# Rows of 256 columns without a gap, and operand tiles at whole 64 bytes, in a one-core encoder block

## The chip, the core and the metric

One core of a Trainium2 chip runs the program. The metric is the device time of one execution in microseconds. Three executions of the kernel before took 1994.06, 1997.44 and 2000.67; the median is 1997.44.

## What is computed

One layer over 256 tokens of width 2048, in float32: two gated feed-forward blocks (FFN) around a token mixer with a convolution group and a gated DeltaNet group. Norms and modulation stand ahead of each.

```python
h = modulate(rmsnorm(x, ffn1_norm[l]), mods[:, 0], mods[:, 1])
x = x + 0.5 * mods[:, 2][:, None, :] * swiglu(h, ffn1_wg[l], ffn1_wu[l], ffn1_wd[l])
h = modulate(rmsnorm(x, mix_norm[l]), mods[:, 3], mods[:, 4])
p = h @ w_in[l]
...
y = jnp.concatenate([y_conv, y_dn], axis=-1) @ w_out[l]
x = x + mods[:, 5][:, None, :] * y
h = modulate(rmsnorm(x, ffn2_norm[l]), mods[:, 6], mods[:, 7])
x = x + 0.5 * mods[:, 8][:, None, :] * swiglu(h, ffn2_wg[l], ffn2_wu[l], ffn2_wd[l])
return rmsnorm(x, final_norm)
```

## The kernel before

All arrays stand transposed: 128 features on the partitions, the 256 tokens along the free axis. A float32 product is made of three float32r matmuls: weights and activations are each split into a leading part (hi) and the rest (lo), and `mm3` (L139) adds hi by hi, hi by lo and lo by hi in PSUM. An activation tile therefore has two rows in a partition, the hi part and the lo part. In `act` tiles (`ffn_evac`, L287) they are two rows of 256 columns, 2048 bytes. In `h` tiles (`h_make` L232, `h_pre` L244, and the mixer's outputs at L568 and L824) they are two rows of 258 columns, 2064 bytes, of which mostly 256 are used; `h_pre` fills the two more with the shift, so that the matmuls of `group` (L260) yield a bias beside the product.

Weights arrive by DMA in `raw` tiles of 1 MB on the queue of SyncE (`load`, L118). `split` (L110) makes of each half a `hi` tile on ScalarE (L113) and a `lo` tile on VectorE (L115); there are four raw, three hi and three lo buffers. One pair of hi and lo carries 24 matmuls.

The stages in order: `first` (L388), the front part of FFN 1, in which the modulation weights still arrive (`ada`, L205) and h is made (L142 to L144, moving operand h); the rest of FFN 1's gate and up products in `col_pair` (L345, matmuls at L354, moving operand h) and its down products (L142 to L144, moving operand act), each in two halves, up to about 790 us; the mixer with `col_tile` (L338, L142 to L144, moving operand h) up to about 1240 us, with small plain float32 matmuls for the DeltaNet (L594 to L818) and seven plain float32 output products (L894); then FFN 2 like FFN 1. Both `group` stages stand at the head of the mixer and of FFN 2, with 258 columns.

The pools stand one behind the other in SBUF: pers, rawp, hip, lop, hp, tmp, small, and behind these the pools of a stage (act tiles, the mixer's tiles). Each tile is rounded up to 32 bytes. What stands in pers is made in `start` (L357), among it `prm` (L368, 593 floats) and the columns `col` and `col2` (L379, L381).

Of the kernel before, what the change touches and what calls it, by code (L numbers as in the profile page):

```python
# [8 lines left out]
F32 = mybir.dt.float32  # L9
F32R = mybir.dt.float32r  # L10
# [5 lines left out]
P = 128  # L16
T = 256
# [23 lines left out]
def spans(items):  # L41
    at, out = 0, {}
    for name, n in items:
        out[name] = slice(at, at + n)
        at += n
    return out, at


PSPAN, NPRM = spans(PARAMS)


class Body:
# [86 lines left out]
    def mm3(self, out, whi, wlo, rhs, start, stop):  # L139
        nc = self.nc  # L140
        rhi, rlo = rhs
        nc.tensor.matmul(out, lhsT=whi, rhs=rhi, start=start, stop=False)  # L142
        nc.tensor.matmul(out, lhsT=whi, rhs=rlo, start=False, stop=False)  # L143
        nc.tensor.matmul(out, lhsT=wlo, rhs=rhi, start=False, stop=stop)  # L144
# [87 lines left out]
    def h_make(self, k, rb, scale, shift, spare=None):  # L232
        nc = self.nc
        sh = self.mods[:, shift * 16 + k:shift * 16 + k + 1]
        h = self.tile(self.hp, [P, 2, T + 2], "h", F32R)
        t = spare() if spare else self.tile(self.tmp, [P, T], "ht")
        nc.vector.scalar_tensor_tensor(out=t, in0=self.x[:, k, :], scalar=self.mods[:, scale * 16 + k:scale * 16 + k + 1],  # L237
                                       in1=rb, op0=ALU.mult, op1=ALU.mult)
        nc.scalar.activation(out=h[:, 0, 0:T], in_=t, func=AF.Identity, bias=sh)
        nc.vector.scalar_tensor_tensor(out=h[:, 1, 0:T], in0=t, scalar=sh, in1=h[:, 0, 0:T].bitcast(F32),  # L240
                                       op0=ALU.add, op1=ALU.subtract)
        self.h[k] = h

    def h_pre(self, k, scale, shift):  # L244

        nc = self.nc
        sc = self.mods[:, scale * 16 + k:scale * 16 + k + 1]
        sh = self.mods[:, shift * 16 + k:shift * 16 + k + 1]
        h = self.tile(self.hp, [P, 2, T + 2], "h", F32R)
        nc.scalar.activation(out=h[:, 0, 0:T], in_=self.x[:, k, :], func=AF.Copy, scale=sc)  # L250
        nc.scalar.activation(out=h[:, 0, T:T + 2], in_=sh.broadcast_to([P, 2]), func=AF.Copy)
        nc.vector.scalar_tensor_tensor(out=h[:, 1, 0:T], in0=self.x[:, k, :], scalar=sc, in1=h[:, 0, 0:T].bitcast(F32),
                                       op0=ALU.mult, op1=ALU.subtract)
        nc.vector.tensor_tensor(out=h[:, 1, T:T + 2], in0=sh.broadcast_to([P, 2]), in1=h[:, 0, T:T + 2].bitcast(F32), op=ALU.subtract)
        self.h[k] = h
# [89 lines left out]
    def col_pair(self, ps, src):  # L345

        nc, kk = self.nc, 0
        for half in range(2):
            for hi, lo in self.weights(src[half]):
                for k in range(4):  # L350
                    rhi, rlo = self.rhs(self.h[kk])
                    for w, r, start, stop in ((hi, rhi, kk == 0, False), (hi, rlo, False, False), (lo, rhi, False, kk == 15)):
                        for g in range(2):
                            nc.tensor.matmul(ps[g], lhsT=w[:, 2 * k + g, :], rhs=r, start=start, stop=stop)  # L354
                    kk += 1

    def start(self):  # L357
        nc, pers = self.nc, self.pers
        self.ones = pers.tile([P, P], F32, name="ones")
        nc.gpsimd.memset(self.ones, 1.0)  # L360
        with self.tc.high_priority():
            nc.scalar.activation(out=self.tile(self.small, [P, 1], "gb", bufs=4), in_=self.ones[:, 0:1], func=AF.Silu)
        c = self.tile(self.rawp, [P, 16, P], "raw").rearrange("p a b -> p (a b)")[0:1, :]
        nc.sync.dma_start(out=c, in_=self.c_d)
        self.x = pers.tile([P, KT, T], F32, name="x")
        for q in range(4):
            nc.sync.dma_start(out=self.x[:, 4 * q:4 * q + 4, :], in_=self.x_d[:, 4 * q:4 * q + 4, :])
        self.prm = pers.tile([P, NPRM], F32, name="prm")  # L368
        nc.sync.dma_start(out=self.prm, in_=self.prm_d)
        self.cb = pers.tile([P, D], F32, name="cb")  # L370
        for i in range(4):
            ps = self.bank(self.auxd)
            nc.tensor.matmul(ps, lhsT=self.ones[0:1, :], rhs=c[:, i * 512:i * 512 + 512], start=True, stop=True)
            nc.scalar.activation(out=self.cb[:, i * 512:i * 512 + 512], in_=ps, func=AF.Silu)
        self.ident, self.upper, self.low = (pers.tile([P, P], F32, name=n) for n in ("ident", "upper", "low"))
        for t, op, sign in ((self.upper, ALU.is_ge, -1), (self.low, ALU.is_gt, 1), (self.ident, ALU.is_equal, 1)):
            nc.gpsimd.affine_select(out=t, in_=self.ones, pattern=[[-sign, P]], compare_op=op, fill=0.0, base=0,
                                    channel_multiplier=sign)
        self.col = pers.tile([P, 1], F32, name="col")  # L379
        nc.gpsimd.memset(self.col, 1.0 / D)  # L380
        self.col2 = pers.tile([P, 1], F32, name="col2")  # L381
        nc.gpsimd.memset(self.col2, 2.0 / D)
        self.mods = pers.tile([P, 144], F32, name="mods")
        self.macc = pers.tile([P, 144], F32, name="macc")
        self.norms.update((n, self.prm[:, PSPAN[n]]) for n in ("n1", "n2", "n3", "nf"))
        self.h = [None] * KT
# [161 lines left out]
    def conv_norm(self):  # L548
        nc = self.nc
        om = self.tile(self.mx, [P, P], "om")  # L550
        nc.gpsimd.memset(om, 2.0 / D)
        pm = self.bank(self.aux)
        nc.tensor.matmul(pm[:, 0:T], lhsT=om, rhs=self.cacc, start=True, stop=True)
        mu = self.tile(self.tmp, [P, T], "rb")
        nc.scalar.activation(out=mu, in_=pm[:, 0:T], func=AF.Copy)
        acc = self.tile(self.tmp, [P, T], "acc", bufs=1)
        for j in range(8):
            nc.vector.tensor_tensor(out=self.cv[j], in0=self.cv[j], in1=mu, op=ALU.subtract)
            self.sq_acc(acc, self.cv[j], j == 0)
            yield 0.7  # L560
        rb = self.token_rsqrt([acc], self.col2)
        yield 3.0
        for j in range(8):
            t = self.cv[j]
            nc.vector.tensor_tensor(out=t, in0=t, in1=rb, op=ALU.mult)
            nc.scalar.activation(out=t, in_=t, func=AF.Silu, scale=self.prm[:, PSPAN["ln_w"]][:, j:j + 1],
                                 bias=self.prm[:, PSPAN["ln_b"]][:, j:j + 1])
            y = self.tile(self.hp, [P, 2, T + 2], "h", F32R)  # L568
            self.put_split(y, t)
            self.y[j] = y  # L570
            yield 0.8
# [238 lines left out]
    def dn_gate(self):  # L810
        nc = self.nc
        for b in range(2):
            O = self.O[b]
            for hp in range(2):
                ps = self.bank(self.aux)
                for i in range(2):
                    for s in range(2):
                        nc.tensor.transpose(out=ps[:, i * T + s * P:i * T + (s + 1) * P], in_=O[s][:, hp * 2 + i, :], identity=self.ident)  # L818
                for i in range(2):
                    h = b * 4 + hp * 2 + i  # L820
                    z = self.zs[h]
                    nc.vector.scalar_tensor_tensor(out=z, in0=ps[:, i * T:(i + 1) * T], scalar=self.prm[:, PSPAN["dn_norm"]], in1=z,
                                                   op0=ALU.mult, op1=ALU.mult)
                    y = self.tile(self.hp, [P, 2, T + 2], "h", F32R)  # L824
                    self.put_split(y, z)
                    self.y[8 + h] = y
                yield 1.5
# [177 lines left out]
```

## Time and profile before

| | |
|---|---|
| median of three executions | 1997.44 us |
| profiled execution, time | 1998.41 us |
| profiled execution, span | 1996.6 us |
| granted TensorE clock, mean | 0.995 |
| busy: PE, DVE, ACT, POOL | 98%, 75%, 46%, 5% |
| DMA | 503.63 MB, mean 252 GB/s |

The span runs from the first to the last instruction of the program; the time of the execution is a little longer. PE is TensorE's matmuls, PEld its loads of weights, DVE VectorE, ACT ScalarE, POOL GpSimd. A matmul's record overlaps the next one, so its mean length is not its cost; the spacing from one to the next is. Busy time is an average over stages.

### The profile page before, as it was taken

To read this page: it belongs to the slowest core of one execution; us is meant where nothing else is said; L and a number is where in the kernel's file an instruction comes from. 1 tells how busy PE (TensorE), PEld (TensorE's weight loads), DVE (VectorE), ACT (ScalarE), POOL (GpSimd) and SP (SyncE) were. 2 spreads that over 40 slices of the span, in tenths; PEclk is the share of its full clock that TensorE was granted. 3 is DMA by queue.
4 is the path that set the end of the run, shared out by engine and by line. 5 is a ranking of instruction groups with operands and counts; after the bars stand their busy time and mean duration, and the time that the engine had idled before them with its cause. 6 is when DMAs were issued, how large, how long until landed. Compare 5 with 4: busy or idle time off the path is not lost.

```text
span 1996.6 us, 38408 instructions
## 1 busy us (share of the span) xinstructions
PE 1950.5 (98%) x16206; PEld 1929.3 (97%) x16206; DVE 1493.5 (75%) x2191; ACT 914.9 (46%) x1298; POOL 99.3 (5%) x192
## 2 busy tenths in 40 slices
PE   5999999999999999999999899999999999999997
PEld 4999999999999999999999899999999999999997
DVE  6879898777878899899999888757665544444554
ACT  3443543334444455754546435544443344444453
POOL 1000000000000000070032300000000000000000
PEclk9999999999999999999999999999999999999998
DMA  8988688888988888447654264567775555555552
GB/s 324 375 342 336 255 334 329 347 324 331 350 319 346 335 336 332 178 176 266 234 201 149 85 253 182 179 231 275 282 269 213 200 187 182 189 188 179 189 199 91
DMA packets 71087, 503.63 MB, mean 252 GB/s; under 512 B 8321, under 2 KB 8961, under 8 KB 10497
## 3 DMA queue, kind: packets, MB, share of 16 engines
q1 hardware_dynamic: 69554, 499.60, 66.3%
q8 instruction: 127, 2.08, 0.4%
q0 software_dynamic: 1360, 1.58, 0.3%
q14 instruction: 46, 0.38, 0.0%
HBM read 498.52 MB, written 2.62 MB: 251 GB/s over the span
## 4 chain that ended last, share of the span: by engine, by line
PE 89%; DVE 4%; POOL 3%; issue 1%; DMA 1%; ACT 1%; DVEq 0%; SPq 0%; ACTq 0%; POOLq 0%
PE ps L354 37%; PE ps L144 16%; PE ps L142 16%; PE ps L143 16%; PE ps L894 3%; DVE lo L115 1%; DMA raw<-in_w_ada 1%; DVE raw L209 1%; PE ps L672 1%; DVE cva L538 1%; POOL dt L506 1%; ACT hi L113 0%; DVE kq L237 0%; POOL cacc L545 0%; DMA x<-in_x 0%
## 5 line engine op out<-in xcount | busy, mean ns | idle before, releaser
L113 ACT ACTIVATE hi<-raw 128x1024 fp32r<-128x1024 f32 x643 | 680.7, 1060 | 949.2 <-PE ps L143 439.3
L115 DVE TENSOR_TENSOR lo<-raw,hi 128x1024 fp32r<-128x1024 f32 x643 | 785.0, 1222 | 422.5 <-ACT hi L113 421.4
L354 PE MATMUL ps<-h,hi 128*128 128x256 f32 x4160 | 664.8, 282 | 0.0
L354 PEld LDWEIGHTS ps<-h,hi 128*128 128x128 f32 x4160 | 567.5, 189 | 0.0
L143 PE MATMUL ps<-h,hi 128*128 128x256 f32 (+1 forms) x1664 | 465.8, 285 | 3.2 <-DVE h L240 3.2
L142 PE MATMUL ps<-h,hi 128*128 128x256 f32 (+1 forms) x1664 | 460.5, 284 | 7.4 <-ACT hi L113 4.1
L144 PE MATMUL ps<-h,lo 128*128 128x256 f32 (+1 forms) x1664 | 446.1, 284 | 1.1 <-DVE lo L115 1.0
L354 PE MATMUL ps<-h,lo 128*128 128x256 f32 x2080 | 414.8, 281 | 0.0
L142 PE MATMUL ps<-act,hi 128*128 128x256 f32 x1408 | 388.2, 277 | 1.0 <-ACT hi L113 1.0
L143 PE MATMUL ps<-act,hi 128*128 128x256 f32 x1408 | 388.1, 277 | 0.0
L144 PE MATMUL ps<-act,lo 128*128 128x256 f32 x1408 | 387.2, 277 | 0.3 <-DVE lo L115 0.3
L209 DVE CUSTOM_DVE_ANT_0 raw<-raw,cb 128x2048 f32<-128x2048 f32 x144 | 328.6, 2284 | 7.8 <-DMA raw<-in_w_ada 7.8
L142 PEld LDWEIGHTS ps<-h,hi 128*128 128x128 f32 x1664 | 313.4, 190 | 9.2 <-ACT hi L113 4.5
L354 PEld LDWEIGHTS ps<-h,lo 128*128 128x128 f32 x2080 | 321.4, 190 | 0.0
L143 PEld LDWEIGHTS ps<-h,hi 128*128 128x128 f32 x1664 | 314.6, 189 | 5.0 <-DVE h L240 3.7
L144 PEld LDWEIGHTS ps<-h,lo 128*128 128x128 f32 x1664 | 303.5, 189 | 3.3 <-DVE lo L115 1.9
L142 PEld LDWEIGHTS ps<-act,hi 128*128 128x128 f32 x1408 | 264.0, 188 | 1.4 <-ACT hi L113 1.4
L144 PEld LDWEIGHTS ps<-act,lo 128*128 128x128 f32 x1408 | 263.4, 188 | 0.7 <-DVE lo L115 0.7
L143 PEld LDWEIGHTS ps<-act,hi 128*128 128x128 f32 x1408 | 263.9, 188 | 0.0
L538 DVE SCALAR_TENSOR_TENSOR cva<-xz,prm,cva 128x251 f32<-128x251 f32 (+15 forms) x240 | 104.6, 476 | 1.2 <-ACT cva L534 0.7
L301 DVE SCALAR_TENSOR_TENSOR x<-ps,mods,x 128x256 f32<-128x256 f32 x96 | 45.9, 479 | 29.2 <-PE ps L144 28.5
L894 PE MATMUL ps<-xz,raw 128*128 128x256 f32 x224 | 51.4, 390 | 0.0
(238 smaller groups left out, 919.2 us busy)
## 6 DMA issues: line engine op xcount, KB each, us to landing
raw<-in_w_ada SPq DMA_DIRECT2D x144, 1024.0 KB, 5.9
raw<-in_gu SPq DMA_DIRECT2D x130, 1024.0 KB, 4.8
raw<-in_wd SPq DMA_DIRECT2D x88, 1024.0 KB, 4.9
raw<-in_w_in SPq DMA_DIRECT2D x42, 1024.0 KB, 5.0
raw<-in_wa SPq DMA_DIRECT2D x40, 1024.0 KB, 8.3
raw<-in_w_out SPq DMA_DIRECT2D x16, 1024.0 KB, 4.9
raw<-in_wk SPq DMA_DIRECT2D x6, 1024.0 KB, 6.3
raw<-in_gw SPq DMA_DIRECT2D x6, 1024.0 KB, 4.9
```

The source lines that it names most:

```text
L113: nc.scalar.activation(out=hi, in_=raw, func=AF.Copy)
L115: nc.vector.tensor_tensor(out=lo, in0=raw, in1=hi.bitcast(F32), op=ALU.subtract)
L142: nc.tensor.matmul(out, lhsT=whi, rhs=rhi, start=start, stop=False)
L143: nc.tensor.matmul(out, lhsT=whi, rhs=rlo, start=False, stop=False)
L144: nc.tensor.matmul(out, lhsT=wlo, rhs=rhi, start=False, stop=stop)
L209: nc.vector.tensor_tensor_reduce(out=w, in0=w, in1=self.cb, scale=1.0, scalar=0.0, op0=ALU.mult, op1=ALU.add, accum_out=self.macc[:, n:n + 1])
L301: self.nc.vector.scalar_tensor_tensor(out=xm, in0=ps, scalar=self.mods[:, gate * 16 + m:gate * 16 + m + 1], in1=xm, op0=ALU.mult, op1=ALU.add)
L354: nc.tensor.matmul(ps[g], lhsT=w[:, 2 * k + g, :], rhs=r, start=start, stop=stop)
L506: nc.gpsimd.tensor_scalar(out=gs[:, i, :], in0=self.low, scalar1=g2[:, b * 4 + i:b * 4 + i + 1], scalar2=None, op0=ALU.mult)
L538: self.taps[j] = nc.vector.scalar_tensor_tensor(out=acc[:, i:T], in0=xs[:, 0:T - i], scalar=w(TAPS - 1 - i), in1=acc[:, i:T], op0=ALU.mult ...
L672: nc.tensor.matmul(ps[:, i * P:(i + 1) * P], lhsT=lhs[:, i, :], rhs=rhs[:, i, :], start=True, stop=True)
L894: nc.tensor.matmul(ps, lhsT=w[:, k, :], rhs=self.zs[k], start=k == 0, stop=k == 7)
```

## The change

`h_tile` makes all h tiles. They become buffers of 528 floats (2112 bytes), and the two rows lie without a gap: 256 columns each, or 258 each in `h_pre`. `prm` is rounded up to 608 floats (2432 bytes), and `col` and `col2` become two columns of one tile of 64 bytes, where each stood in a tile of its own. No instruction is added or removed.

```diff
     def h_make(self, k, rb, scale, shift, spare=None):
-        h = self.tile(self.hp, [P, 2, T + 2], "h", F32R)
+        h = self.h_tile()
...
+    def h_tile(self, extra=0):
+
+        n = T + extra
+        return self.tile(self.hp, [P, 2 * T + 16], "h", F32R)[:, 0:2 * n].rearrange("p (g t) -> p g t", g=2)
+
     def h_pre(self, k, scale, shift):
...
-        h = self.tile(self.hp, [P, 2, T + 2], "h", F32R)
+        h = self.h_tile(2)
...
-        self.prm = pers.tile([P, NPRM], F32, name="prm")
+        self.prm = pers.tile([P, -(-NPRM // 16) * 16], F32, name="prm")[:, 0:NPRM]
...
-        self.col = pers.tile([P, 1], F32, name="col")
+        cols = pers.tile([P, 16], F32, name="col")
+        self.col, self.col2 = cols[:, 0:1], cols[:, 1:2]
         nc.gpsimd.memset(self.col, 1.0 / D)
-        self.col2 = pers.tile([P, 1], F32, name="col2")
         nc.gpsimd.memset(self.col2, 2.0 / D)
...
-            y = self.tile(self.hp, [P, 2, T + 2], "h", F32R)
+            y = self.h_tile()
             self.put_split(y, t)
...
-                    y = self.tile(self.hp, [P, 2, T + 2], "h", F32R)
+                    y = self.h_tile()
                     self.put_split(y, z)
```

## Rows read from the trace of the kernel before

**Rows 1.** The page: busy time of the engines, and the chain that ended last.
```profile
PE 1950.5 (98%) x16206; PEld 1929.3 (97%) x16206; DVE 1493.5 (75%) x2191; ACT 914.9 (46%) x1298; POOL 99.3 (5%) x192
...
PE 89%; DVE 4%; POOL 3%; issue 1%; DMA 1%; ACT 1%; DVEq 0%; SPq 0%; ACTq 0%; POOLq 0%
PE ps L354 37%; PE ps L144 16%; PE ps L142 16%; PE ps L143 16%; PE ps L894 3%; DVE lo L115 1%; DMA raw<-in_w_ada 1%; DVE raw L209 1%; PE ps L672 1%; DVE cva L538 1%; POOL dt L506 1%; ACT hi L113 0%; DVE kq L237 0%; POOL cacc L545 0%; DMA x<-in_x 0%
```

**Rows 2.** The page's costliest groups, the splits: busy us, mean ns, idle before, releaser.
```profile
L113 ACT ACTIVATE hi<-raw 128x1024 fp32r<-128x1024 f32 x643 | 680.7, 1060 | 949.2 <-PE ps L143 439.3
L115 DVE TENSOR_TENSOR lo<-raw,hi 128x1024 fp32r<-128x1024 f32 x643 | 785.0, 1222 | 422.5 <-ACT hi L113 421.4
```

**Rows 3.** Waits of PE: us in total, times, longest.
```profile
PE ps L198 <- ACT dg L194: 8.7, 1, 8.7
PE ps L818 <- ACT A L806: 5.5, 1, 5.5
PE ps L142 <- ACT hi L113: 5.1, 4, 2.3
...
PE ps L749 <- ACT R L738: 0.2, 1, 0.2
```

**Rows 4.** The chain in order of time: start us, us, what, how many.
```profile
418.03 251.39 PE ps L354 x2112
...
1028.41 1.78 PE ps L672 x16
...
1143.91 0.44 PE ps L818 x4
1144.35 16.41 PE ps L894 x76
...
1274.47 216.73 PE ps L354 x1823
1610.88 251.38 PE ps L354 x2112
```

**Rows 5.** Windows: length, busy us and count by engine, clock, DMA share, GB/s.
```profile
50.00:100.00 50.00, 46.29 (x382) 45.48 (x381) 44.56 (x57) 22.73 (x29) 0.00 (x0) 1.00 0.96 375
100.00:266.00 166.00, 166.00 (x1401) 166.00 (x1399) 142.60 (x196) 77.98 (x102) 0.00 (x0) 1.00 0.79 305
315.00:415.00 100.00, 99.75 (x847) 99.54 (x846) 81.05 (x92) 37.16 (x35) 0.00 (x0) 1.00 0.89 351
672.00:780.00 108.00, 108.00 (x956) 108.00 (x955) 99.78 (x147) 54.35 (x83) 0.00 (x0) 1.00 0.90 349
850.00:900.00 50.00, 48.35 (x388) 46.00 (x387) 45.16 (x92) 26.86 (x43) 36.47 (x69) 1.00 0.51 183
900.00:1000.00 100.00, 100.00 (x846) 100.00 (x845) 92.57 (x165) 48.66 (x64) 3.01 (x6) 1.00 0.68 247
1000.00:1100.00 100.00, 99.85 (x860) 99.64 (x860) 94.78 (x172) 59.26 (x108) 29.55 (x38) 1.00 0.49 174
1100.00:1150.00 50.00, 44.33 (x299) 40.98 (x299) 45.01 (x112) 20.46 (x60) 18.95 (x50) 0.93 0.24 85
1500.00:1600.00 100.00, 100.00 (x885) 100.00 (x884) 51.08 (x52) 38.72 (x38) 0.00 (x0) 1.00 0.55 202
```

**Rows 6.** Timeline of PE, two places: start us, us, line, tiles.
```profile
710.06 0.28 PE L142 MATMUL ps<-act,hi 128*128 128x256 f32 x1
...
710.74 0.28 PE L143 MATMUL ps<-act,hi 128*128 128x256 f32 x1
...
802.46 0.59 PE L198 MATMUL ps<-dg,ones 128*128 128x256 f32 x2
```

**Rows 7.** Groups of PE, shapes apart: count, busy us, mean ns.
```profile
L354 PE MATMUL ps<-h,hi 128*128 128x256 f32 x4160 | 664.8, 282 | 0.0
L354 PE MATMUL ps<-h,lo 128*128 128x256 f32 x2080 | 414.8, 281 | 0.0
L143 PE MATMUL ps<-h,hi 128*128 128x256 f32 x1456 | 408.5, 285 | 3.2 <-DVE h L240 3.2
L142 PE MATMUL ps<-act,hi 128*128 128x256 f32 x1408 | 388.2, 277 | 1.0 <-ACT hi L113 1.0
L142 PE MATMUL ps<-h,hi 128*128 128x258 f32 x192 | 52.9, 285 | 0.0
L672 PE MATMUL ps<-dt,dt 128*128 128x128 f32 x96 | 12.7, 275 | 0.0
```

**Rows 8.** Groups of DVE at L237: count, busy us, mean ns.
```profile
L237 DVE SCALAR_TENSOR_TENSOR hq<-x,mods,rb 128x256 f32<-128x256 f32 x16 | 6.9, 473 | 0.0
L237 DVE SCALAR_TENSOR_TENSOR kq<-x,mods,rb 128x256 f32<-128x256 f32 x16 | 6.5, 480 | 0.0
```

**Rows 9.** Groups of PE from 1250 to 1274 us, L198 alone.
```profile
L198 PE MATMUL ps<-dg,ones 128*128 128x256 f32 x2 | 0.6, 378 | 0.0
```

## Prediction

> **What bounds the kernel now.** I read the page first. TensorE is busy 98% of the span, and its work is 89% of the chain that ended last, 37% of it at L354 alone [rows 1]. That is not yet proof, since a busy PE can be a slow PE. So I looked at who waits for whom: before its splits ScalarE idles 949 us, mostly released by PE at L143, and VectorE idles 422 us, released by ScalarE [rows 2]. The engines that feed TensorE wait for TensorE to give buffers back. TensorE's own waits come to about 37 us, the longest of them once 8.7 us at the start [rows 3]. What is left is the spacing from one matmul to the next, and the reader is to see there that it is not one number.
>
> I divide stretches by their counts. L354 (h as moving operand) runs 2112 matmuls in 251.39 us of the chain, 119.0 ns each, and the other two long rows of it give 118.9 and 119.0 [rows 4]. In a window a matmul's record of 0.28 us reaches over the edges, so about 2.4 of the count are too many. The h matmuls of L142 to L144 then take 166/(1401 - 2.4) = 118.7 ns from 100 to 266 us and 118.5 from 900 to 1000. The same three lines with an act tile as moving operand take 108/(956 - 2.4) = 113.3 ns from 672 to 780 and 113.3 from 1500 to 1600 [rows 5]; in the timeline six of them take 0.68 us [rows 6]. The function, the 256 columns, the weights tiles and the granted clock (1.00 in these four windows, the level of 2.4 GHz) are the same. So 5.3 to 5.7 ns a matmul hang on the moving tile, on a path that is 89% PE. One stretch breaks the pattern: act from 315 to 415 us takes 100/(847 - 2.4) = 118.4 ns [rows 5], on the same buffers as 672 to 780.
>
> **What differs is the place.** In the built program of before, prm (593 floats, 2372 bytes) pushes all that follows off: raw, hi, lo and act begin 32 bytes past a multiple of 64; h tiles (2064 bytes, placed every 2080) begin in turn at 0 and 32; their second row, 1032 bytes on, begins at 8 or 40. After: prm takes 2432 bytes, everything to act moves to multiples of 64, h is placed every 2112 and its second row, 1024 on, also begins at a multiple of 64.
>
> **What size to expect.** 113.3 ns at 2.4 GHz is 272 cycles, 256 columns and 16 more; 64 bytes are 16 such columns. I take this as the hypothesis that a row which begins within a 64-byte block costs one block more. Streams whose operands do begin at multiples of 64 exist here, in plain f32: L672 takes 1.78/16 = 111.3 ns, L818's transposes 0.44/4 = 110 [rows 4]. They have other passes, so they are the nearest rows and no proof. For the spacing of aligned fp32r I take 111.3, with 110 below and act's own 113.3 above as bounds. The relation of weights to moving rows stays what act has now (both at the same place modulo 64), which is why I take act as the upper bound.
>
> **The sum, part by part** (counts from [rows 7], lines split by stage as the loops say).
> - L354: 4160 + 2080 = 6240, 119.0 to 111.3: 7.7 ns, 48.0 us.
> - First stage, 1401 of its 1920 matmuls (the rest lies before 100 us, where DMA ends last, and counts nothing): 7.4 ns, 10.4 us.
> - Mixer: 4368 - 1920 + 48 = 2496: 7.3 ns, 18.2 us.
> - The 3 x 192 matmuls of 258 columns: their second row still begins 1032 bytes on, at 8. I count 0; bounded by 576 x 5.7 = 3 us either way.
> - act: 2816 (three halves) x 2.0 = 5.6 us; 1408 (first half of FFN 1) x 7.1 = 10.0 us.
>
> Gross 92 us. Some is given back. From 850 to 1150 us VectorE is busy 277.6 of 300 us [rows 5]; some 1700 of the 2393 matmuls counted there are h's and would gain 12, and VectorE's fixed work allows that only without a gap, so I take off 6. From 315 to 415 the DMA moves 351 GB/s; 6% more is 373, and the most that any window has is 375 [rows 5]: I take off 4 there, and 2 in the first stage. Net 80.
>
> Costs beside the path: VectorE's and ScalarE's instructions keep their shapes. L237 reads and writes tiles at 0 (kq) in 480 ns and at 32 (hq) in 473 [rows 8], no gain to see; 32 such instructions make under 1 us, beside matmuls. The small f32 tiles of the mixer (kq, xz, dt, L, A) go the other way, from 0 to 32, since one 32-byte tile lies ahead of them. If that cost a block (6.7 ns) on the 224 of L894 and about 340 smaller ones (L672's 96 the largest group [rows 7]) it were 4 us. But L198's moving tile lies at 32 now and two of its matmuls take 0.59 us [rows 6]; less the 0.38 that one lasts [rows 9] that leaves 0.21 between the two, against 215.9 ns for L894 at 0 [rows 4]. I count nothing. Transfers now land at multiples of 64; DMA is 1% of the chain [rows 1], so 5% on it is 1 us either way.
>
> The profiled execution took 1998.4 us, its span 1996.6, the median of three is 1997.4. 1998.4 - 80 = 1918.
>
> **Two rules beside the rows.** The spacing of h and of act differs by 5.7 ns [rows 4, 5]. The Trainium skill (TensorE: Matmul & The Clock Gate, Back-to-back issue gap) gives N/2.4 + 2.5 ns, 109 for 256 columns, with no term for the address; by it nothing here changes and the time stays 1998 (rival 4). The trace disagrees, 113 and 119. The rows of h lie at 0, 8, 32 and 40 and those of act at 32 alone. The Trainium skill (SBUF — State Buffer, Specifications) has lines of 16 bytes, each crossing to a new one paying; by it only the second rows of h begin within a line, and act has nothing to gain: 1942, the first rival below. What the trace has against it: it leaves act's 272 cycles unexplained.
>
> **The rivals.**
> 1. *Only evenness counts.* h becomes as regular as act, and neither goes below 113.3. L354 5.7 x 6240 = 35.6, first stage 5.4 x 1401 = 7.6, mixer 5.3 x 2496 = 13.2, first half of FFN 1 5.1 x 1408 = 7.2 if it lands in act's usual spacing: 64, less 8 given back: 1942. For it: half of the h tiles begin at 0 already, and L354 stays at 119 [rows 4]. Against: the even 272.
> 2. *A slower step.* Act has two steady spacings, 113.3 and 118.4, on the same addresses [rows 5], so a weight load and a matmul can fall into step in a worse way and stay there. If aligned streams stay in a step about 5 ns worse, h runs at 116.3 (2.8 x 10137 = 28 us gained, 3 more in the first half of FFN 1) and the other act halves lose 3 x 2816 = 8: 1975.
> 3. *The slower step without a gain (slower than before).* The same mechanism with no block saved: with both operands at the start of a block, every fetch of weights meets one of the moving row. All act halves run at 118.4 (5.1 x 2816 = 14.4 us lost), h at 118.4 (0.3 to 0.6 ns, 5 us gained): 2008. It decides from h at about 117.5 on, with act above 118.
> 4. *The place doesn't matter* and h differs from act by something else: 1998. For it, the 118.4 of act at act's own addresses. Against, that L142 to L144 are the same code for both.
>
> **How the numbers follow.** Forecast 0.46, rival 1 0.27, rival 2 0.11, rival 3 0.08, rival 4 0.08. The predicted time is the forecast's, 1918. Its best bound is 110 ns: 6240 x 9.0 + 1401 x 8.7 + 2496 x 8.6 + 2816 x 3.3 + 1408 x 8.4 = 111 us with nothing given back, 1887. The range 1890 to 1975 takes in the forecast, rival 1 and rival 2. A measurement of this kernel tells about 0.3% (6 us) from no change; rivals 1 and 2 are faster by that, so faster 0.84, same 0.08, slower 0.08.
>
> **What would show it.** Chain rows of 2112 at L354 in about 235 us (251.4 now); 239 speaks for rival 1, 246 for rival 2. The act window from 1500 on at about 900 matmuls in 100 us for the forecast, 885 for rival 1, under 850 for rivals 2 and 3. PE's waits on VectorE should grow between 850 and 1150, and DMA's share should near 0.95 around 350 us; if the first 300 us wait for DMA, the give-back was too small. The 258-column matmuls should stay. The prediction is wrong if L354 keeps 119, or if h falls and the end doesn't.

## The result, and the profile after

| | before | after |
|---|---|---|
| median of five executions each, us | 1998.93 | 2007.67 |
| ratio, 95% interval | 1 | 1.0051 (1.004 to 1.0062) |
| span of the profiled execution, us | 1996.6 | 2005.7 |

The change makes the kernel 0.5% slower. 1918 was forecast, in a range of 1890 to 1975; the forecast, its range and its sign were wrong. Rival 3 had named 2008.

The page of after, engines and chain, answers to [rows 1], and the two groups of the splits to [rows 2]:

```profile
PE 1961.4 (98%) x16206; PEld 1940.1 (97%) x16206; DVE 1494.4 (75%) x2191; ACT 914.8 (46%) x1298; POOL 98.2 (5%) x192
...
PE 93%; DVE 4%; POOL 1%; ACT 1%; issue 1%; DMA 0%; SPq 0%; DVEq 0%; ACTq 0%; POOLq 0%
...
L113 ACT ACTIVATE hi<-raw 128x1024 fp32r<-128x1024 f32 x643 | 680.6, 1060 | 961.5 <-PE ps L143 488.6
L115 DVE TENSOR_TENSOR lo<-raw,hi 128x1024 fp32r<-128x1024 f32 x643 | 784.9, 1222 | 427.9 <-ACT hi L113 426.6
```

Nothing is new beside TensorE: VectorE and ScalarE do the same work in the same time, and wait a little longer: ScalarE for TensorE, VectorE for ScalarE. What answers to [rows 4] is the chain of after in order of time (start us, us, what; the pair loop of L354 is L359 now):

```profile
415.85 250.53 PE ps L359 x2112
...
1275.56 216.22 PE ps L359 x1823
1616.15 250.51 PE ps L359 x2112
```

L359 gained 0.9 us in either row of 2112, where the forecast had 16. The shorter row of FFN 2, 1823 matmuls, gained 0.5. What answers to [rows 5] is the windows of after (length; busy us and count of PE, PEld, DVE, ACT, POOL; clock; DMA share; GB/s):

```profile
100.00:266.00 166.00, 166.00 (x1412) 166.00 (x1411) 144.17 (x198) 78.71 (x103) 0.00 (x0) 1.00 0.80 310
315.00:415.00 100.00, 100.00 (x852) 100.00 (x851) 80.34 (x90) 37.16 (x35) 0.00 (x0) 1.00 0.89 351
672.00:780.00 108.00, 108.00 (x920) 108.00 (x918) 96.71 (x138) 52.40 (x81) 0.00 (x0) 1.00 0.88 338
900.00:1000.00 100.00, 100.00 (x843) 100.00 (x842) 92.33 (x164) 48.21 (x63) 3.23 (x8) 1.00 0.67 249
1500.00:1600.00 100.00, 100.00 (x852) 100.00 (x851) 49.02 (x51) 37.99 (x36) 0.00 (x0) 1.00 0.54 195
```

The act stretches from 672 and from 1500 us fell from 956 to 920 and from 885 to 852 matmuls, at the same granted clock of 1.00. That is the loss. From here on spacings are taken from start to start of the matmuls' records, counted against the program's own list of matmuls; they repeat to 0.01 ns within a steady stretch. In ns a matmul, h in the first stage, at L354 in FFN 1 and FFN 2 (stretches well inside), in the mixer from 905 to 995 us, and act in its four halves:

| kernel | h first | h L354 | h mixer | act FFN 1 | act FFN 2 | median us |
|---|---|---|---|---|---|---|
| before | 118.7 | 119.0, 119.0 | 118.6 | 117.8, 113.3 | 113.3, 113.3 | 1998.9 |
| after | 117.7 | 118.6, 118.6 | 118.9 | 117.8, 117.8 | 117.8, 117.8 | 2007.7 |

The account: three halves of act, 3168 matmuls, by 4.44 ns are 14.1 us lost; the mixer's 2496 by 0.3 lose 0.7. L354 gains 2.3 (6240 by about 0.4) and the first stage 1.4 (1401 by 1.0). 11.1 us remain; the spans differ by 9.1, and the rest are small waits (PE's on the hi splits 5.1 to 4.5 us, on the lo splits 1.3 to 0.6) and eight matmuls more done before 100 us.

Three numbers return in many stretches: 113.33, 117.78 and 120.00 ns, which are 272, 282.67 and 288 cycles at 2.4 GHz. The question was what chooses among them. Four theories stood: the place of an operand modulo 64 (as rival 3 has it); the distance of the moving row from the weights tile; history, that is two possible steps, of which one is taken as a stretch begins and is then kept (a step is here the even spacing of a stretch); and the forecast's saved block, which act had already refuted.

What put the distance on the list is after's own trace. All its operands begin at multiples of 64, and h is still uneven. Its tiles stand every 2112 bytes, 64 more than a multiple of 256, and the weights every 512, so from one h tile to the next the distance walks by 64 modulo 256. Sorted by it, the mean gaps behind an h matmul were 119.8 ns at 0, 118.0 at 64, 119.3 at 128 and 116.8 at 192. Act's tiles stand every 2048 bytes; its distance is 64 throughout, before and after. That the period is 256 and not 512 bytes shows in the same trace: between tile k and tile k + 4 the distance moves by 256, and their mean gaps agree (at L359 in FFN 1, from the first tile on: 120.3, 116.8, 119.1 and 118.3 ns, then 120.3, 116.8, 119.0 and 118.4).

### The profile page after: what moved, and what is told of

Read it like the earlier page. It is cut to its first block, busy times and chain, and to the rows that moved or that the text cites. A ratio compares the mean times of both kernels' runs of the same rounds, so it can differ in the third digit from the quotient of the medians.

```text
span 2005.7 us, 38408 instructions
## 1 busy us (share of the span) xinstructions
PE 1961.4 (98%) x16206; PEld 1940.1 (97%) x16206; DVE 1494.4 (75%) x2191; ACT 914.8 (46%) x1298; POOL 98.2 (5%) x192
## 4 chain that ended last, share of the span: by engine, by line
PE 93%; DVE 4%; POOL 1%; ACT 1%; issue 1%; DMA 0%; SPq 0%; DVEq 0%; ACTq 0%; POOLq 0%
PE ps L359 37%; PE ps L142 17%; PE ps L144 17%; PE ps L143 17%; PE ps L899 2%; DVE cva L543 1%; DVE lo L115 1%; PE ps L677 1%; DVE raw L209 0%; DMA x<-in_x 0%; DVE kq L237 0%; ACT hi L113 0%; PE ps L599 0%; POOL cacc L550 0%; PE ps L186 0%
## 5 line engine op out<-in xcount | busy, mean ns | idle before, releaser
L359 PE MATMUL ps<-h,hi 128*128 128x256 f32 x4160 | 665.5, 282 | 0.0
L359 PEld LDWEIGHTS ps<-h,hi 128*128 128x128 f32 x4160 | 570.7, 189 | 0.0
L359 PE MATMUL ps<-h,lo 128*128 128x256 f32 x2080 | 413.4, 280 | 0.0
L359 PEld LDWEIGHTS ps<-h,lo 128*128 128x128 f32 x2080 | 315.4, 188 | 0.0
```

## The experiments

### Each half of the change alone

**Only the rows.** The kernel before with the new `h_tile`, `prm` and `col` left alone:

```diff
-        h = self.tile(self.hp, [P, 2, T + 2], "h", F32R)
+        h = self.h_tile()
...
+        return self.tile(self.hp, [P, 2 * T + 16], "h", F32R)[:, 0:2 * n].rearrange("p (g t) -> p g t", g=2)
```

> Only the gapless rows of h in buffers of 2112 bytes; prm and the two columns stay as before, so weights, h and act all begin 32 bytes past a multiple of 64. Place theory (operands at multiples of 64 stay in the slower step, operands 32 bytes past one take the faster): h, now evenly placed, and act both at 113.3 ns a matmul, about 1940 us. Distance theory (what counts is the distance of the moving row from the weights tile modulo 256 bytes, which steps by 64 from one h tile to the next): h at 118 to 119 ns in L354's chain rows, 2112 matmuls in 249.5 to 251.5 us; act not decided by it, since act's distance is the same in the kernels before and after: each of the four halves at 113.3 or at 117.8, so 1994 us with three or four fast halves, 2008 with none. History theory (one of two steps is taken as a stretch begins and kept): as distance theory for h, act mixed from half to half.

**Only the places.** The kernel before with `prm` of 608 floats and `col`, `col2` in one tile of 64 bytes:

```diff
-        self.prm = pers.tile([P, NPRM], F32, name="prm")
+        self.prm = pers.tile([P, -(-NPRM // 16) * 16], F32, name="prm")[:, 0:NPRM]
...
```

> Only prm and the columns rounded up: weights and act begin at multiples of 64, h tiles keep their rows of 258 columns and begin in turn at 32 and 0. Place theory: act at 117.8 ns in all four halves, three of them slower by 4.4 ns than before, 14 us, about 2012 us; h unchanged at 118.9. Distance theory: h's distances only change their order, 119 ns, act not decided, 1994 to 2012 us. History theory: act mixed from half to half, 1998 to 2012 us, and another execution may have another mix.

The rows alone took 2009.65 us (1.005, 1.0035 to 1.0065), the places alone 2000.54 (1.0, 0.9991 to 1.0009). The act window from 672 us, first of the rows alone, then of the places alone:

```profile
672.00:780.00 108.00, 108.00 (x919) 108.00 (x919) 96.73 (x139) 52.42 (x81) 0.00 (x0) 1.00 0.87 338
```

```profile
672.00:780.00 108.00, 108.00 (x955) 108.00 (x955) 100.12 (x144) 53.56 (x83) 0.00 (x0) 1.00 0.90 350
```

The reader is to see that 955 is before's 956 with every operand of act at a multiple of 64, and that 919 is after's 920 with every one 32 bytes past it. So the place modulo 64 does nothing, and the whole loss comes from the h tiles, though it falls on act. Over the four halves of act the places alone repeat before (117.8, then three times 113.3) and the rows alone repeat after (four times 117.8). The place theory is out, and with it rival 3's reason.

### One distance for each stage

All h tiles in one region, every 2048 bytes, so that the distance stays constant in a stage: 0 for FFN 1's h, 128 in the mixer, 192 in FFN 2.

```diff
...
-        return self.tile(self.hp, [P, 2 * T + 16], "h", F32R)[:, 0:2 * n].rearrange("p (g t) -> p g t", g=2)
+        at = 64 + k * 2 * n if extra else k * 2 * T + (self.off if off is None else off)
+        return self.hb[:, at:at + 2 * n].rearrange("p (g t) -> p g t", g=2)
...
```

> The change, and all h tiles in one region, one every 2048 bytes, so that the distance of the moving row from the weights tile modulo 256 bytes is constant in a stage: 0 for h of the first stage and of FFN 1, 128 for the mixer's h, 192 for FFN 2's h and act, 64 for FFN 1's act. All at multiples of 64. Distance theory, from the mean gaps of the four distances in the changed kernel (119.8, 118.0, 119.3 and 116.8 ns for 0, 64, 128 and 192): FFN 1's h at 119.8 or more, the mixer at 119.3, FFN 2's h and act under 117, so L354 in FFN 2 under 247 us for 2112 (250.5 in the changed kernel) and in FFN 1 over 252; about 1995 us in all. With a constant distance each may settle into an even step of its own, 113.3 for 192. Place theory: 117.8 everywhere, about 2000. First forecast (a row at the start of a block saves one): 111.3 everywhere, refuted already by act.

> As the run at multiples of 64 with constant distances, but with everything 32 bytes past a multiple of 64; the distances are the same. Distance theory: the same spacing in each stage as there, within 0.5 ns. Place theory: 113.3 ns in every stage, about 1925 us. History theory: stages differ between the two runs without a rule.

They took 2014.32 and 2014.95 us, and every steady stretch agrees between the two within 0.02 ns. The chain of the run at multiples of 64, L354's long rows (L360 here):

```profile
419.88 253.44 PE ps L360 x2112
1285.35 214.71 PE ps L360 x1823
1624.43 248.75 PE ps L360 x2112
```

At 0 the spacing is exactly 120.00 (253.44/2112), at 192 it is 117.78 (248.75/2112). The distance counts, then, but the theory had 113.3 or under 117 for 192, and act, now at 192 in FFN 2, kept 117.78 too. The expected total of 1995 was missed by 19 us for that reason. A constant distance isn't enough.

### Matmuls alone

Three programs held only matmuls, in blocks, on constant tiles: no DMA, VectorE or ScalarE beside them. Each ran once; the third has pauses between some blocks, in which TensorE waits for ScalarE. In some blocks the matmuls go by pairs, as at L354: each of the three products for two weights in turn.

> Only matmuls, nothing else of the layer: 13454 fp32r matmuls on constant tiles with 128 columns of weights and 256 moving columns, in blocks of 96 or 192, with no DMA, VectorE or ScalarE beside them; the list of blocks runs forward and then backward, so each block has two different predecessors. Blocks differ in the distance of the moving row from the weights tile (0 to 224 bytes modulo 256), in the distance of the second row from the first (1024, 1028, 1032, 1040, 1056, 1088, 1152), in the order (three products in turn, or pairs as in L354), in a stride of 2048, 2080 or 2112 from tile to tile, in a single shorter matmul ahead, and in where the lo weights stand. The time itself (about 1.6 ms) says nothing; the spacing of each block does. Distance theory: one spacing for each distance, 120.0 for 0 and 117.8 for 64, 128 and 192, in both directions. History theory: the blocks named act (distance 64, second row 1024 on) at 113.3 behind a block with second rows 1032 on, as before's act behind its h, and at 117.8 behind blocks of even rows, as in the changed kernel; and a single shorter matmul ahead can change the spacing of all that follow. If all blocks are at 117.8 to 120 whatever came ahead, 113.3 needs something that this kernel doesn't have (writes into SBUF beside the matmuls, or the place of the tiles beyond 256 bytes).

The timeline of the first of them, in three blocks, by starts of the hi products (start us, us): distance 0, then 64, then 64 again at the end of the program; nine matmuls lie between the two starts of a pair.

```profile
71.73 0.40 PE L91 MATMUL ps<-act,hi 128*128 128x256 f32 x2
...
72.81 0.40 PE L91 MATMUL ps<-act,hi 128*128 128x256 f32 x2
...
94.77 0.40 PE L91 MATMUL ps<-act,hi 128*128 128x256 f32 x2
...
95.83 0.40 PE L91 MATMUL ps<-act,hi 128*128 128x256 f32 x2
...
1577.73 0.39 PE L91 MATMUL ps<-act,hi 128*128 128x256 f32 x2
...
1578.76 0.39 PE L91 MATMUL ps<-act,hi 128*128 128x256 f32 x2
```

1.08, 1.06 and 1.03 us: over the whole blocks 120.00, 117.78 and 113.33. The second and the third are the same block with the same addresses; only what ran ahead differs (distance 32 there, 96 here). So writes beside the matmuls aren't needed for any of the three steps. Distance 0 was at 120.00 whatever came ahead. Distance 64 with its second row 1024 bytes on was at 117.78 in nearly all blocks, whatever row spacing or shorter matmul came first, and distance 192 at 113.33 or 117.78. The expectation that a row 1032 on would by itself lead act into 113.3 was wrong: behind such blocks act was at 117.78.

> Only matmuls again: for every combination of three distances in steps of 64 bytes (row 1 from the hi weights, row 2 from row 1 less 1024, lo weights from the hi weights; 64 combinations) four blocks of 60 matmuls in an order by chance, so that each has four different predecessors. The spacing of each block's second half is read. Distance theory: the four blocks of a combination agree. Distance and history: some combinations have two spacings (64, 0, 0 and 192, 0, 0 had 113.3 and 117.8 in the run before this), others one; 0, 0, 0 always 120.0; a combination with 113.3 in all four is what a kernel should be laid out for (64, 0, 128 had it twice).

Of the 64 layouts 23 had blocks that differ by more than 0.3 ns, so history is common; all 256 blocks lie between 113.33 and 121.13, at 118.1 in the mean. Some layouts, named by three distances in bytes modulo 256 (first row from the hi weights, second row from the first less 1024, lo weights from the hi weights):

| layout | its four blocks, ns |
|---|---|
| 192, 0, 128 | 113.3, 113.3, 113.3, 113.4 |
| 64, 0, 128 | 113.3, 118.9, 113.3, 118.9 |
| 192, 0, 0 | 113.3, 117.8, 117.8, 117.8 |
| 64, 0, 0 (act here) | 117.8, 117.8, 117.8, 117.8 |
| 128, 0, 0 | 120.0, 118.7, 118.7, 120.0 |
| 0, 0, 0 | 120.0, 120.0, 120.0, 120.0 |

One layout had 113.3 alone: lo weights half of 256 bytes off the hi weights, moving rows at 192.

> Only matmuls: 22 layouts, each six times behind 24 matmuls of another layout chosen by chance and twice behind a pause in which TensorE waits for ScalarE. Distance and history: 192, 0, 128 at 113.3 in all eight in the order of mm3; its order by pairs is open (113.3 if only the set of distances counts); 64, 0, 0 and 192, 0, 0 split between 113.3 and 117.8 by what came ahead; 64, 0, 128 between 113.3 and 118.9. Layouts 8 or 16 bytes off 192 show whether the distance has to be exact. If each layout has one spacing whatever came ahead, history is out.

192, 0, 128 was at 113.33 in all eight, and in all eight by pairs too. 64, 0, 0 took 113.33 twice and 117.78 six times, 192, 0, 0 five and three times, 64, 0, 128 five times 113.33 and three times 118.89. The distance has to be exact: at 184 and 200, 8 bytes off, the step was 120.0, at 176 117.8, at 208 mostly 118.8.

### History inside the kernel

```diff
-        return self.tile(self.hp, [P, 2 * T + 16], "h", F32R)[:, 0:2 * n].rearrange("p (g t) -> p g t", g=2)
+        return self.tile(self.hp, [P, 2 * T + 4], "h", F32R)[:, 0:2 * n].rearrange("p (g t) -> p g t", g=2)
```

This is the run of the rows alone with smaller buffers, so that every tile stays where it stood before.

> The kernel before with one thing changed: the second row of each h tile begins 1024 bytes behind the first, not 1032; the tiles keep their places every 2080 bytes, and the weights and act tiles stand at the same addresses as before, byte for byte. History theory: act now begins behind h with other gaps, so its halves can fall from 113.3 to 117.8 ns although nothing of act is moved: 0 to 3 halves of some 1056 matmuls, 4.7 us each, on an h between 117 and 119.5 ns. If act's own addresses decide: the same as before, 118 in the first half and 113.3 in the other three.

It took 1993.33 us (0.9983, 0.9974 to 0.9992). Its windows, in act's four halves, two in the first:

```profile
290.00:303.00 13.00, 13.00 (x117) 13.00 (x116) 12.74 (x22) 6.42 (x12) 0.00 (x0) 1.00 0.79 314
318.00:400.00 82.00, 82.00 (x699) 82.00 (x698) 66.10 (x74) 30.79 (x29) 0.00 (x0) 1.00 0.91 345
690.00:770.00 80.00, 80.00 (x682) 80.00 (x681) 71.89 (x105) 38.99 (x61) 0.00 (x0) 1.00 0.85 324
1515.00:1595.00 80.00, 80.00 (x708) 80.00 (x707) 40.29 (x41) 31.74 (x30) 0.00 (x0) 1.00 0.56 198
1885.00:1965.00 80.00, 80.00 (x708) 80.00 (x707) 44.62 (x52) 40.00 (x51) 0.00 (x0) 1.00 0.47 170
```

Weights and act are at before's addresses, byte for byte. Yet the half from 690 us, at 113.33 before, has 682 matmuls in 80 us (117.78), where FFN 2's halves have 708 (113.33). The first half begins at 113.36, keeps 113.33 behind a wait of TensorE for a lo split at 305.3 us, and goes on at 117.77 behind two waits for hi splits:

```profile
309.40 0.39 PE L142 MATMUL ps<-act,hi 128*128 128x256 f32 x1 [0.58 <-ACT hi L113]
...
310.35 0.38 PE L142 MATMUL ps<-act,hi 128*128 128x256 f32 x1 [0.44 <-ACT hi L113]
```

Before's own first half holds both steps on the same addresses: 117.76 up to 307.8 us, 113.33 in the 25 matmuls from 308.3, and 117.78 from 316.7 on. So what runs ahead of an act stretch decides its step, and a wait can decide it anew. That the total came out below before is mostly h, 118.0 at L354 and 117.5 in the mixer here; nobody chose these values.

### The way out, and its counter-proof

First the smallest step: after, with 128 bytes of padding ahead of the lo tiles, which puts act at 192, 0, 128.

```diff
+        self.pad = pool("pad", 1)
         self.lop = pool("lop", 3)
...
+        nc.gpsimd.memset(self.tile(self.pad, [P, 32], "pad"), 0.0)
```

> The changed kernel with 128 bytes of padding ahead of the lo tiles and nothing else: h walks by 64 bytes from tile to tile as in the changed kernel, act gets the layout of 192, 192 and 64. Distance and history: act at 113.3 in all four halves, 4224 by 4.4 ns, 19 us less than the changed kernel if h stays, so about 1989 us; h walks through 192, 64, 128 and 0 with lo half a period off, mean of these in the run on all distances 113.3, 118.9, 118.4 and 119.1, so about 117.5 against 118.6, 8 to 12 us more gained: 1977 to 1989. If an even h ahead always leads act into 117.8: 2008.

It took 1987.96 us (0.996 of before, 0.9944 to 0.9975), at the upper end of the 1977 to 1989 expected. Act is at 113.33 in all four halves, behind h with rows 1024 bytes apart, which in after led into 117.78, and behind the waits of the first half too; h, still walking, kept 118.3 at L354 and did not gain the 8 to 12 us more. The same window as above, 956 again:

```profile
672.00:780.00 108.00, 108.00 (x956) 108.00 (x954) 100.16 (x145) 53.41 (x83) 0.08 (x1) 1.00 0.89 347
```

Then all of it: the region of h tiles every 2048 bytes, and h and act at 192 in every stage (the offset of 48 counts floats; each pad holds 32).

```diff
+        self.pad = pool("pad", 1)
         self.lop = pool("lop", 3)
+        self.pad2 = pool("padb", 1)
...
-        self.off = 0
+        self.off = 48
...
-        with tc.tile_pool(name="actp", bufs=FH) as self.actp, tc.tile_pool(name="spp", bufs=2) as self.spp, \
+        with tc.tile_pool(name="pad1", bufs=1) as pad1, tc.tile_pool(name="actp", bufs=FH) as self.actp, tc.tile_pool(name="spp", bufs=2) as self.spp, \
```

> The layout that had one spacing only, 113.3, in the run on all distances: row 1 at 192 from the hi weights, row 2 1024 on, the lo weights 128 bytes off the hi weights, so that the three products of mm3 stand at 192, 192 and 64. Made from the run with constant distances at 32: h and act at 192 in every stage, 128 bytes of padding ahead of the lo tiles. If distance and history set the spacing and nothing else does: 113.3 ns in the first stage, the mixer and all four halves of act whatever came before; L354, whose order by pairs was not among those blocks, at 113.3 too or at one of 115 to 119. Gain against before: L354 6240 by 5.6 ns, first stage 1401 by 5.4, mixer 2496 by 5.3, the first half of FFN 1 1056 by 5.0, in all 61 us, less some 8 where other engines or the DMA are near their limit: about 1945 us; with L354 unchanged about 1978. If writes into SBUF beside the matmuls or the weights' absolute place matter as well: some halves at 117.8, 1960 to 2000.

1948.45 us, 0.9739 of before (0.9718 to 0.976), 3.5 us from the 1945 expected; it beats both kernels. Its chain and windows (the pair loop is L362):

```profile
407.60 239.36 PE ps L362 x2112
...
1248.01 206.64 PE ps L362 x1823
1574.33 239.36 PE ps L362 x2112
```

```profile
50.00:100.00 50.00, 44.61 (x366) 44.02 (x365) 42.27 (x55) 21.72 (x29) 0.00 (x0) 0.93 0.94 358
100.00:266.00 166.00, 166.00 (x1467) 166.00 (x1466) 149.56 (x205) 82.89 (x109) 0.00 (x0) 1.00 0.82 324
315.00:400.00 85.00, 85.00 (x753) 85.00 (x752) 70.44 (x78) 33.60 (x32) 0.00 (x0) 1.00 0.90 353
1460.00:1550.00 90.00, 90.00 (x796) 90.00 (x796) 47.70 (x49) 35.31 (x34) 0.00 (x0) 1.00 0.58 207
```

239.36/2112 is 113.33; 1467 stand where before had 1401 and after 1412. Every stretch of 256 columns that doesn't wait runs at 113.33, h like act. The gross gain is 61 us (L354 35, first stage 7.5, mixer 13, first half of FFN 1 5), the net 49: PE's waits for the splits are longer, and the window from 50 us holds 366 matmuls for 382 before: TensorE waited 4.2 us for a hi split until 71.5 us, and its granted clock in the ten us from 70 was 0.66, where before had 1.00. Most of what is missing, 9 us, is in the mixer: from its first matmul to FFN 2's first at L362 it shrank from 485.0 to 481.0 us only, where 13 stood.

```profile
PE ps L144 <- ACT hi L115: 7.3, 4, 4.2
...
PE ps L146 <- DVE lo L117: 4.8, 6, 2.4
```

Together 12.1 us, against 6.4 before (5.1 on hi, [rows 3], and 1.3 on lo).

The counter-proof moves h by 8 bytes in that kernel (the mixer's outputs too, from an offset of 112 to 114), and nothing else:

```diff
-        self.off = 48
+        self.off = 50
```

> The kernel with 192 and lo half a period off, all h tiles 8 bytes further (200), act left at 192. Matmuls alone took 120.0 at 200 where 192 took 113.3. Distance theory: L354's, the first stage's and the mixer's h at 120.0, 6.67 ns on some 10000 matmuls: 60 to 66 us slower than without the shift, about 2010 us; act stays at 113.3. If only the multiples of 64 count: 1948.

2015.24 us in two executions, 66.8 more. The mixer's h went to 120.0, the first stage's to 120.4, L354's by pairs to 121.1; act stayed at 113.33 (954 in the window from 672 us, where the 8 bytes don't reach it).

```profile
425.00:660.00 235.00, 235.00 (x1943) 235.00 (x1942) 182.62 (x215) 97.66 (x121) 0.00 (x0) 1.00 0.87 330
672.00:780.00 108.00, 108.00 (x954) 108.00 (x954) 99.39 (x135) 52.99 (x71) 0.00 (x0) 1.00 0.90 349
```

The 8 bytes also take the rows off every multiple of 16, so this run alone doesn't tell the distance from a rule of 16 bytes. Two others do: at 176 and 208, whole multiples of 16, matmuls alone were at 117.8 and 118.8, and places moved by 32 bytes at constant distances changed nothing.

## Why the prediction was wrong, point by point

**The bound was right.** TensorE's spacing bounds the kernel [rows 1 to 5]: where it changed the end moved by about as much, and where it improved everywhere, 49 of 61 us arrived.

**The step that failed is "What size to expect".** It took 272 cycles as 256 columns and a block, and let a row at a multiple of 64 save the block: 111.3. After the change h stood at 117.7 to 118.9 and act at 117.8. The runs showed no effect of the place modulo 64 at all (places alone, 2000.5; the two runs with constant distances, 0.6 us apart). The nearest rows it leaned on, L672 and L818, are plain float32 with other passes, and the step itself said they were no proof. No layout of the 64 went below 113.33.

**"What differs is the place" read the wrong modulus.** It compared each tile's place with multiples of 64. What the runs showed in its place is the distance of the moving row from the weights modulo 256, for hi and lo apart. By that measure after's h isn't even: 2112 bytes make the distance walk. L354 accordingly went from 119.0 to 118.6, and not to 111 or, as rival 1 had it, 113.3.

**The upper bound of act failed, and it cost the sign.** The sum gave act 2.0 ns in three halves and 7.1 in one, with its own 113.3 as the worst, since its relation to the weights stays. The relation did stay, but act has two steps on it, 113.33 and 117.78. The rows said so: 315 to 415 us at 118.4 and 672 to 780 at 113.3, same buffers, same clock [rows 5]. Two spacings on the same addresses cannot be a function of the address. That row was read as a stretch to be gained, not as a step into which the others could fall. (The window had a short wait in it; the step itself is 117.78.)

**The counts of act were mis-split.** All act matmuls are 4224, in four halves of 1056. The sum has 2816 for three halves and 1408 for the first; it should be 3168 and 1056. In the forecast this moves 2 us, it turns rival 3's loss of 14.4 into 16.2.

**Rival 3 had the time, not the reason.** 2008 against 2007.7, with h at 118.6 as it asks and act at 117.8, just under the 118 it named. That the time fits to 0.3 us is luck: its 14.4 us come from a loss of 5.1 ns (measured 4.44) on 2816 matmuls (3168), and of the 5 us that it let h gain 3 came. Its mechanism, that both operands at the start of a block meet at every fetch, is refuted: the rows alone, with all operands 32 bytes past, lose the same. What held is what it borrowed from rival 2, that a stretch falls into a slower step on the same addresses and stays there; that it is a weight load and a matmul that fall into step was not shown. Rival 2 itself missed (1975) because it kept the saved block under its slower step. With the two steps seen in the rows, 0.08 for rival 3 was too little.

**Rivals 1 and 4.** Evenness alone is not what makes 113.3, for h at a constant distance stood at 120.00 and 117.78; rival 1's 1942 was the right size for a layout that the change didn't make (1948). Of rival 4 the first half held, that the place modulo 64 doesn't matter; a spacing free of the address is refuted by 8 bytes that cost 66.8 us.

**Right beside it:** the 258-column matmuls stayed (their records 285 ns before and after), and the give-back of 12 us for a faster TensorE was in all what the kernel at 113.33 paid, though there 9 of it were the mixer's, not 6. In after, with nothing gained, neither VectorE's waits nor the DMA share grew.

**The two rules.** The runs find 272 cycles as the least spacing of these streams, and up to 291 on other layouts (121.13 ns). The Trainium skill (TensorE: Matmul & The Clock Gate, Back-to-back issue gap) lists 262 cycles for 256 columns, without the address, and as the gap of an isolated matmul, not of a stream of weight loads and matmuls. The prediction held it against streams, so their 113 and 119 ns don't contradict it; the spacings of the 64 layouts lie 10 to 29 cycles above it. The lowest and the highest of the 64 layouts differ by 7.8 ns by distance alone. The Trainium skill (SBUF — State Buffer, A bandwidth-pool intuition that's wrong) gives the weights load a second independent read port. By it one would expect the distance not to matter; here it does, by the 7.8 ns.

**What stays open.** Why the spacing hangs on the distance modulo 256, why some layouts have two steps and 192, 0, 128 only one, was not shown; no run looks below the matmul's start. Each kernel was traced once; that the steps are not drawn by lot from execution to execution rests on the two pairs of runs that repeat each other's four halves, and on the times (after's five lie within 1.9 us, where one half of act is worth 4.7). Nor was it settled what in the last h matmuls ahead of act picks the step: in matmuls alone rows 1032 bytes apart did not lead into 113.33, in the kernel before they mostly did.

## What to carry to other kernels

Divide stretches by their counts and compare the spacing of one instruction form from stage to stage: two spacings at one granted clock, on the same addresses, are two states, and a change anywhere ahead can flip them. Where TensorE bounds, lay out weights and moving rows by their distance modulo 256 bytes, keep tile strides at multiples of 256, and try all distances in one program of matmuls alone before touching the kernel; choose a layout that has one step from every predecessor. Rounding to multiples of 64 is no substitute: by itself it did nothing here, and with a stride of 2112 the distance still walked.

## What the runs showed of the hardware

- fp32r matmuls of 256 columns with 128-column weights in steady streams take exact steps, 113.33, 117.78 and 120.00 ns among them, which depend on the distance of moving row and weights modulo 256 bytes and not on the place modulo 64.
- Several layouts have two steps and keep the one that they entered; waits for hi splits changed it (113.33 ns up to 308.5 us, 117.77 from 310.9 us, act's addresses unchanged), and a wait at 305.3 us did not.
- Lo weights 128 bytes off the hi weights, moving rows at 192 from hi: 113.33 in all 20 blocks, in both orders, and in every stage of the kernel. 8 bytes off: 120.0 ns in matmuls alone, 66.8 us in the kernel.
